# Weight sums of the banded attention's gates in tiles of a pool, loaded sooner, and a difference of tokens formed later

## The chip, the cores and the metric

The kernel runs on one core of one Trainium2 chip. The metric is device microseconds (us) of one execution. TensorE (PE) multiplies, ScalarE (ACT) and VectorE (DVE) work element by element, GpSimd (POOL) mostly issues transfers that add to what is in memory, and SyncE (SP) issues the plain loads. Each engine works through its own instructions in a fixed order.

## The reference, cut to what matters

One decoder layer, for 512 tokens of width 1024. Three branches read the same normalised tokens, and each is scaled by a sigmoid gate that is a projection of those tokens too:

```
u = rms_norm(h, ln_mix_pre)
qa, ka, va, qb, kb, vb, qm, gl = split(u @ w_in)      # gl: 3 x 1024 gate columns
y_swa = banded attention with sinks (8 heads of 64, window 128, relative bias)
y_sb  = stick-breaking attention   (8 heads of 64)
y_mem = attention over 256 memory rows (4 heads of 128)
g = sigmoid(gl)
merged = g[0] * (y_swa @ w_swa) + g[1] * (y_sb @ w_sb) + g[2] * (y_mem @ w_mem)
h = h + rms_norm(merged @ w_out)
h = h + rms_norm(swiglu(rms_norm(h)))
```

The banded attention's softmax is taken over the 256 keys of two neighbouring blocks, with a maximum that includes the sink; the first block of tokens has no block before it, and its weights there are zero.

## The kernel before, in words

**Products.** Everything stays close to fp32. An operand is split into a rounded part `hi` and a remainder `lo`, and each product is three matmuls, hi·hi, lo·hi and hi·lo (`mm3`, L190, whose three lines are L192, L194 and L195). `hi` is a cast on ACT (L146, L149 with a sign), `lo` a subtraction on DVE (L147, L150). For a few weights `lo` is made by ACT (L170) and a transfer of POOL that adds the weights from memory to it (L171).

**The stream.** Weights of 128 rows by 1024 come in the order of a list of units (`Stream`). When unit k starts on PE, `ahead` (L67) issues the loads up to unit k+4 on SP, and the splits up to unit k+3. Raw weights lie in a ring of five tiles (`raw`), hi and lo in rings of four. With a load or a split a unit can carry further steps ("load", "after"). A list of matmuls is fed bit by bit between the steps of the attention: `dn.run(us)` emits so many us of it.

**The gates of the banded attention.** They are made with seven products in place of eight half-size ones. `quarter` (L451) computes for each half n of the columns the products p1, p2 and p4 with plain weights, and p5, p6, p3 and p7 with sums of weights: "s" (for p5, then with more added for p6, then for p3) and "t" (for p7). A sum is made in a raw tile: `q_raw` (L391) loads it on SP, and `q_plus` (L398) adds to it by a transfer of POOL. `add_two_groups` (L482) lists the 14 units in the order p1, p5, p2, p6, p7, p3, p4, each with n = 0 and 1, and hangs those loads and additions at units some places ahead. Names: qx and qy are PSUM tiles of these products, qw a sum's tile, qkp a product copied out of PSUM (L438).

**The right sides.** The products need differences of tokens too. `rights` (L504) is a generator. Its first part takes the sum of hi and lo of the tokens of both halves, and their difference, in four tiles fx (L515, L516, on DVE); its second part splits the differences back into n0h to n3l, in place; later parts make the right sides of p6, p7 and p4.

**The banded attention.** `swa_pair` (L935) does two heads, four times (c = 0 to 3). Scores are in PSUM. POOL sets the first 128 columns of w to a large negative number (L954); DVE adds the bias (L955 to L957), takes the maxima (L965) and combines them with the sink (L968); ACT takes the exponentials, four of 128x256 and one of 128x4 for each head; DVE divides (L973 to L977); PE transposes (L988), ACT and DVE copy the transposes out of PSUM (L990, L991), and PE multiplies by the values (ysw, L198). Beside pairs 0 and 1 runs the stick-breaking branch's product with its weights (br, L192 to L195, with a gate's multiplication at L645), beside the last pairs the query projection of the memory heads (qm, evacuated by ACT at L327), and behind them the gates' products.

The program's order on each engine follows from the order of the code, a scheduler's priorities and what is ready in its own account; the rows under the change show what came out.

Of the kernel before, what the change touches and what calls it, by code (L numbers as in the profile page):

```python
# [14 lines left out]
ALU = mybir.AluOpType  # L15
# [99 lines left out]
def tile_kernel(ctx, tc, a):  # L115
    nc = tc.nc

    base = ctx.enter_context(tc.tile_pool(name="base", bufs=1))
# [10 lines left out]
    def ck(name, dt=F32):  # L129
        return ckp.tile([P, 512], dt, tag="ck", name=name)  # L130
# [12 lines left out]
    def split(raw, hi, lo, sign=1.0):  # L143

        if sign == 1.0:
            ins = nc.scalar.copy(hi, raw)  # L146
            lows = nc.vector.tensor_tensor(lo, raw, hi.bitcast(F32), op=ALU.subtract)  # L147
        else:
            ins = nc.scalar.mul(hi, raw, sign)  # L149
            lows = nc.vector.scalar_tensor_tensor(lo, raw, sign, hi.bitcast(F32), op0=ALU.mult, op1=ALU.subtract)  # L150
        if "behind" in st:
            after(ins, st["behind"][0])
            after(lows, st["behind"][1])
        return ins
# [12 lines left out]
    def split_dma(raw, hi, lo, src):  # L167

        nc.scalar.copy(hi, raw)
        nc.scalar.mul(lo, hi.bitcast(F32), -1.0)  # L170
        nc.gpsimd.dma_start(like(lo, src), src, accum_op=ALU.add)  # L171

    def w_split(raw, n, src=None):
        uid[0] += 1
        hi = wp.tile([P, 1024], F32R, tag="hi", name=f"hi{uid[0]}", bufs=4)
        lo = wp.tile([P, 1024], F32R, tag="lo", name=f"lo{uid[0]}", bufs=4)
        if src is not None:
            split_dma(raw[:, :n], hi[:, :n], lo[:, :n], src)
            return hi, lo
        sign = 1.0  # L180
        if isinstance(raw, tuple):
            raw, sign = raw
        ins = split(raw[:, :n], hi[:, :n], lo[:, :n], sign)
        if "chain" in st:
            after(ins, st["chain"])
        return hi, lo

    dn = Stream(w_load, w_split)

    def mm3(out, l, r, start, stop, right_last=False):  # L190
# [9 lines left out]
    def cols(hl, o, n):  # L200
        return hl[0][:, o : o + n], hl[1][:, o : o + n]
# [3 lines left out]
    def after(ins, first):  # L205
        dep = mybir.DependencyInfo(mybir.DependencyClass.NoSync, mybir.DependencyReason.DATA)
        tc.add_manual_dep(ins.ins, first.ins.name, dep, reason="order")
# [171 lines left out]
    qw, qb_, qk = {}, {}, {}  # L379
# [8 lines left out]
    def q_src(b, n, f, j):  # L388
        c = 17 + 8 * b + 4 * f + 2 * n
        return a["w_p"][:, c : c + 2, 4 * j : 4 * j + 4].rearrange("p g k n -> p g (k n)")  # L390
# [7 lines left out]
    def q_plus(b, n, key, f, j):  # L398
        raw = qw[(b, n, key)]
        nc.gpsimd.dma_start(raw[:, :].rearrange("p (g m) -> p g m", g=2), q_src(b, n, f, j), accum_op=ALU.add)  # L400

    def q_got(b, n, p):
        key = {"p5": "s", "p6": "s", "p3": "s", "p7": "t"}.get(p, p)

        def got():
            if (b, n, key) not in qw:
                q_raw(b, n, key, *{"p1": (0, 0), "p2": (0, 1), "p4": (1, 1)}[p])
            raw = qw[(b, n, key)]
            return (raw, -1.0) if p == "p3" else raw

        return got
# [39 lines left out]
    def quarter(b, n, p):  # L451
        def gen(hi, lo):
            if p in ("p1", "p5", "p2"):
                bank = aps if p == "p5" or (b, p) == (SWA, "p2") else dps
                qb_[(b, n, TILE[p])] = bank(f"q{TILE[p]}{b}{n}")
            ps = qb_[(b, n, TILE[p])]
            for j in range(2):
                for k in range(4):
                    first = p in ("p1", "p5", "p2") and j == 0 and k == 0
                    mm3(  # L460
                        ps[:, j * 256 : (j + 1) * 256], cols((hi, lo), (j * 4 + k) * P, P), right_of(p, k), first, k == 3
                    )
                    yield 0.36
            q_end(b, n, p, ps)

        return gen
# [14 lines left out]

    def add_two_groups(b):  # L482

        order = [(n, p) for p in ("p1", "p5", "p2", "p6", "p7", "p3", "p4") for n in range(2)]
        base = len(dn.units)
        for n, p in order:
            if p in PLAIN:
                dn.add(q_src(b, n, *PLAIN[p]), 1024, quarter(b, n, p))
            else:
                dn.add(q_got(b, n, p), 1024, quarter(b, n, p))  # L490

        def load_with(unit, back, *args):
            dn.units[base + order.index(unit) - back]["load"].append(lambda: args[0](*args[1:]))

        for n in range(2):
            load_with((n, "p5"), 4, q_raw, b, n, "s", 1, 0)
            load_with((n, "p5"), 2, q_plus, b, n, "s", 1, 1)
            load_with((n, "p7"), 4, q_raw, b, n, "t", 1, 0)
            load_with((n, "p7"), 3, q_plus, b, n, "t", 0, 0)
        for n in range(2):  # L500
            for p, j in (("p5", 0), ("p6", 1)):
                dn.units[base + order.index((n, p))]["after"].append(lambda n=n, j=j: q_plus(b, n, "s", 0, j))

    def rights():  # L504

        x, y = {}, {}

        def part(p, k, src, sign):
            h, l = cols(right[p][k // 2], (k % 2) * 256, 256)
            split(src, h, l, sign)  # L510

        for k in range(4):
            x[k] = ck(f"fx{k}")
            a0, a1 = x[k][:, :256], x[k][:, 256:]
            nc.vector.tensor_tensor(x[k][:, :], u[k][0].bitcast(F32), u[k][1].bitcast(F32), op=ALU.add)  # L515
            nc.vector.tensor_tensor(a1, a1, a0, op=ALU.subtract)  # L516
        yield
        for k in range(4):
            split(x[k][:, 256:], u[k][0][:, 256:], u[k][1][:, 256:])
        dn.open()  # L520
        yield
        for p in ("p6", "p7", "p4"):
            right[p] = [(ck(f"{p}rh{c}", F32R), ck(f"{p}rl{c}", F32R)) for c in range(2)]
        for k in range(4):
            y[k] = ck(f"fy{k}")
            b1 = y[k][:, 256:]
            nc.vector.tensor_tensor(y[k][:, :], u[4 + k][0].bitcast(F32), u[4 + k][1].bitcast(F32), op=ALU.add)
            nc.vector.tensor_tensor(b1, x[k][:, 256:], b1, op=ALU.subtract)
            part("p6", k, b1, 1.0)
            yield  # L530
        for p, z in (("p7", x), ("p4", y)):
            for k in range(4):
                b0 = z[k][:, :256]
                nc.vector.tensor_tensor(b0, y[k][:, 256:], b0, op=ALU.add)
                part(p, k, b0, -1.0)
                if k % 2:
                    yield
# [125 lines left out]
    for h in range(2):  # L663
        for q in range(3):
            n = 3 if q < 2 else 2
# [30 lines left out]
    dn.mark("plain_end")  # L696
    dn.gate()
    add_two_groups(SWA)
    dn.mark(f"gates{SWA}")
    add_branch(SWA, 1, False)  # L700
# [122 lines left out]
    def band_bias():  # L823
        oh = ck("oh")
        nc.gpsimd.dma_start(oh[:32, :384], a["onehot"])
        rbt = ck("rbt")
        nc.gpsimd.dma_start(rbt[:32, :8], a["rel_bias"])
        wm = ck("wm")
        nc.gpsimd.dma_start(wm[:, :384], a["winmask"])

        rb16 = ck("rb16")
        nc.gpsimd.tensor_copy(
            rb16[:32, :P].rearrange("b (h j) -> b h j", h=8), rbt[:32, :8].unsqueeze(2).to_broadcast([32, 8, 16])
        )
        ps = aps("pbias")
        mm(ps[:, :384], rb16[:32, :P], oh[:32, :384], True, True)
        row = ck("brow")
        nc.vector.tensor_tensor(row[:, :384], ps[:, :384], wm[:, :384], op=ALU.add)
        scr = drm.tile([8, P * 384], F32, name="bscr")
        nc.gpsimd.dma_start(  # L840
            scr[:, :].rearrange("h (j m i) -> (h j) m i", j=16, m=8),
            row[:, :384].unsqueeze(1).to_broadcast([P, 8, 384]),
        )
        out = []
        for i in range(4):
            b = ck(f"bias{i}")
            src = scr[2 * i : 2 * i + 2, 127:383]
            src = bass.AP(src.tensor, src.offset, [[383, P], [P * 384, 2], [1, 256]])
            nc.gpsimd.dma_start(b[:, :].rearrange("p (h k) -> p h k", h=2), src)
            out.append(b)  # L850
        return out
# [189 lines left out]
    for h in range(8):  # L1041
        if h == 1:
            bias = band_bias()
# [6 lines left out]
    dn.open()  # L1050
    table("natural_log_exp_and_others")
    for c in range(4):
        for us in swa_pair(c, bias):
            dn.run(us)
        if c == 2:
            made = rights()
            next(made)
    dn.until("plain_end")
    for _ in made:
        dn.run(1.5)  # L1060
# [607 lines left out]
```

## Time and profile before

| | |
|---|---|
| median of 3 runs | 811.78 us (811.72 to 812.59) |
| profiled execution | 810.99 us |
| its span | 809.2 us |
| granted TensorE clock | 0.997 of 2.4 GHz |
| PE busy | 796.1 us, 98% of the span |
| DVE, ACT, POOL busy | 76%, 60%, 12% |

The span runs from the first to the last instruction that the trace holds; the profiled execution is 1.8 us longer than its span. A row of a timeline begins with the start within the span, then the time that the instruction (or xN of them) took; what stands in brackets is the idle time of the engine before it, and what ended it. The stretch that the change touches lies between 200 and 330 us.

### The profile page before, as it was taken

What the parts mean: (1) busy time and instruction counts of PE and PEld (TensorE: products, weight loads), DVE (VectorE), ACT (ScalarE), POOL (GpSimd) and SP (SyncE); (2) the same over time, 40 slices, a digit from 0 to 9 for tenths busy, and PEclk for the clock granted to TensorE, in tenths of its full rate; (3) what the DMA queues carried; (4) which work ended last, traced back from release to release, by engine and by line L of the source; (5) the groups of instructions that cost most, each with busy time, mean ns of one, the idle gap of its engine ahead of it and who ended that gap; (6) DMA issues with size and microseconds to landing.
All of it is one profiled execution on the core that took longest, in us unless ns stands there. A gap on an engine that the chain in (4) does not pass through costs nothing.

```text
span 809.2 us, 13115 instructions
## 1 busy us (share of the span) xinstructions
PE 796.1 (98%) x5011; PEld 711.2 (88%) x5011; DVE 611.8 (76%) x985; ACT 487.1 (60%) x882; POOL 93.2 (12%) x115
## 2 busy tenths in 40 slices
PE   9999999999999999999999999999999999999996
PEld 6899788878788789889988899999999999988885
DVE  6898678545267787696694869967676777898797
ACT  7466677666856574755562566654444444666573
POOL 1002110000211111100004200100000000205200
PEclk9999999999999999999999999999999999999998
DMA  9343455213877438705569925987777662759902
GB/s 312 124 147 104 134 165 158 78 52 95 171 152 157 78 80 211 179 1 157 168 235 317 220 50 142 275 208 200 192 174 196 176 168 83 178 133 224 207 1 104
DMA packets 45295, 125.57 MB, mean 155 GB/s; under 512 B 5008, under 2 KB 6560, under 8 KB 45232
## 3 DMA queue, kind: packets, MB, share of 16 engines
q1 hardware_dynamic: 32368, 88.30, 33.5%
q0 software_dynamic: 12432, 36.17, 24.9%
q8 instruction: 39, 0.64, 0.3%
q10 hardware_dynamic: 432, 0.27, 0.1%
q14 instruction: 24, 0.20, 0.1%
HBM read 121.04 MB, written 3.67 MB: 154 GB/s over the span
## 4 chain that ended last, share of the span: by engine, by line
PE 91%; DVE 4%; DMA 1%; ACT 1%; issue 1%; DVEq 0%; ACTq 0%
PE gx L195 5%; PE gx L192 5%; PE gx L194 5%; PE z L198 4%; PE br L194 3%; PE br L192 3%; PE br L195 3%; PE x L194 2%; PE x L192 2%; PE x L195 2%; PE gy L195 2%; PE gy L194 2%; PE gy L192 2%; PE g L192 2%; PE g L194 2%; PE mx L192 2%
## 5 line engine op out<-in xcount | busy, mean ns | idle before, releaser
L146 ACT CAST hi<-gw 128x1024 fp32r<-128x1024 f32 x77 | 79.8, 1048 | 81.4 <-DVE gw L1253 39.8
L147 DVE TENSOR_TENSOR lo<-gw,hi 128x1024 fp32r<-128x1024 f32 x77 | 93.6, 1223 | 34.0 <-ACT hi L146 33.9
L146 ACT CAST hi<-raw 128x1024 fp32r<-128x1024 f32 (+2 forms) x46 | 46.7, 1028 | 40.9 <-PE qb L194 11.3
L147 DVE TENSOR_TENSOR lo<-raw,hi 128x1024 fp32r<-128x1024 f32 (+2 forms) x46 | 55.8, 1217 | 12.5 <-ACT hi L146 12.3
L1235 POOL DMA_DIRECT2D gw<-in_w_gu x27 | 23.3, 897 | 190.6 <-DMA gw<-in_w_gu 91.0
L146 ACT CAST hi<-r 128x1024 fp32r<-128x1024 f32 (+1 forms) x24 | 23.6, 982 | 19.9 <-PE y L195 5.3
L194 PE MATMUL x<-lo,lh 128*128 128x512 f32 x88 | 34.2, 389 | 0.0
L192 PE MATMUL x<-hi,lh 128*128 128x512 f32 x88 | 34.2, 389 | 0.0
L195 PE MATMUL x<-hi,ll 128*128 128x512 f32 x88 | 34.1, 389 | 0.0
L147 DVE TENSOR_TENSOR lo<-r,hi 128x1024 fp32r<-128x1024 f32 (+1 forms) x24 | 27.2, 1133 | 3.8 <-ACT hi L146 3.7
L892 DVE SCALAR_TENSOR_TENSOR e<-z,e 128x384 f32<-128x384 f32 (+1 forms) x24 | 14.4, 599 | 20.0 <-ACT e L211 20.0
L147 DVE TENSOR_TENSOR lo<-qw,hi 128x1024 fp32r<-128x1024 f32 x18 | 22.0, 1220 | 8.9 <-ACT hi L146 8.9
L211 ACT ACTIVATE e<-e 128x384 f32<-128x384 f32 (+1 forms) x48 | 26.9, 561 | 1.5
L400 POOL DMA_DIRECT2D qw<-in_w_p x12 | 14.5, 1245 | 114.8 <-DVE lo L147 34.7
L146 ACT CAST hi<-qw 128x1024 fp32r<-128x1024 f32 x18 | 18.9, 1050 | 14.1 <-PE qx L194 3.6
L146 ACT CAST hi<-bp 128x512 fp32r<-128x512 f32 x33 | 19.2, 620 | 13.5 <-PE y L195 4.8
L195 PE MATMUL gx<-N2h,lo 128*128 128x256 f32 x88 | 25.0, 284 | 0.3 <-DVE lo L147 0.3
L192 PE MATMUL gx<-B11h,hi 128*128 128x256 f32 x88 | 25.1, 285 | 0.2 <-ACT B11h L1164 0.2
L147 DVE TENSOR_TENSOR lo<-bp,hi 128x512 fp32r<-128x512 f32 x33 | 21.5, 686 | 4.7 <-ACT hi L146 4.5
L192 PE MATMUL mx<-woh,mgh 128*128 128x512 f32 x64 | 25.0, 391 | 0.0
L195 PE MATMUL gw<-B21h,lo 128*128 128x256 f32 x88 | 25.0, 284 | 0.0
L194 PE MATMUL gx<-B11l,hi 128*128 128x256 f32 x88 | 25.0, 284 | 0.0
(924 smaller groups left out, 3042.3 us busy)
## 6 DMA issues: line engine op xcount, KB each, us to landing
gw<-in_w_gu SPq DMA_DIRECT2D x57, 512.0 KB, 5.2
raw<-in_w_p SPq DMA_DIRECT2D x28, 512.0 KB, 4.3
gw<-in_w_gu POOLq DMA_DIRECT2D x27, 512.0 KB, 7.3
qw<-in_w_p SPq DMA_DIRECT2D x14, 512.0 KB, 4.6
raw<-in_w_br SPq DMA_DIRECT2D x12, 512.0 KB, 4.2
qw<-in_w_p POOLq DMA_DIRECT2D x12, 512.0 KB, 6.1
bp<-in_w_dn SPq DMA_DIRECT2D x22, 256.0 KB, 8.4
r<-in_w_dn POOLq DMA_DIRECT2D x10, 512.0 KB, 8.4
```

Of the source, the lines that this page charges most:

```text
L146: ins = nc.scalar.copy(hi, raw)
L147: lows = nc.vector.tensor_tensor(lo, raw, hi.bitcast(F32), op=ALU.subtract)
L192: one = nc.tensor.matmul(out, lh, rh, start=start, stop=False, skip_group_check=True)
L194: nc.tensor.matmul(out, *two, start=False, stop=False, skip_group_check=True)
L195: return one, nc.tensor.matmul(out, *three, start=False, stop=stop, skip_group_check=True)
L198: return nc.tensor.matmul(out, l, r, start=start, stop=stop, skip_group_check=True)
L211: ins = nc.scalar.activation(*args, **kw)
L400: nc.gpsimd.dma_start(raw[:, :].rearrange("p (g m) -> p g m", g=2), q_src(b, n, f, j), accum_op=ALU.add)
L892: nc.vector.scalar_tensor_tensor(x, z[i][:, :n], 0.0, x, op0=ALU.max, op1=ALU.add)
L1235: nc.gpsimd.dma_start(gw[(n, key)][:, :], g_src(n, i, j), accum_op=ALU.add)
```

## The change

The units of the banded gates come in the order (0,p1), (1,p1), (0,p2), (0,p5), (1,p5), (1,p2), then as before. The sum "s" of each half lies in two 128x512 tiles of the general pool (`ck`) instead of one 128x1024 tile of the raw ring; its loads, additions and splits are two each, of half the size. They are issued one unit (load) and two units (first addition) further ahead of p5. `rights()` is begun after the softmax of the last pair was emitted, not after pair c = 2. `w_split` takes a list of tiles.

```
--- before.py
+++ after.py
@@ -180,7 +180,11 @@
         sign = 1.0
         if isinstance(raw, tuple):
             raw, sign = raw
-        ins = split(raw[:, :n], hi[:, :n], lo[:, :n], sign)
+        if isinstance(raw, list):
+            for i, x in enumerate(raw):
+                ins = split(x[:, :], hi[:, i * 512 : (i + 1) * 512], lo[:, i * 512 : (i + 1) * 512], sign)
+        else:
+            ins = split(raw[:, :n], hi[:, :n], lo[:, :n], sign)
         if "chain" in st:
             after(ins, st["chain"])
         return hi, lo
@@ -481,7 +485,8 @@
 
     def add_two_groups(b):
 
-        order = [(n, p) for p in ("p1", "p5", "p2", "p6", "p7", "p3", "p4") for n in range(2)]
+        order = [(0, "p1"), (1, "p1"), (0, "p2"), (0, "p5"), (1, "p5"), (1, "p2")]
+        order += [(n, p) for p in ("p6", "p7", "p3", "p4") for n in range(2)]
         base = len(dn.units)
         for n, p in order:
             if p in PLAIN:
@@ -492,14 +497,22 @@
         def load_with(unit, back, *args):
             dn.units[base + order.index(unit) - back]["load"].append(lambda: args[0](*args[1:]))
 
+        def s_raw(n):
+            qw[(b, n, "s")] = [ck(f"qs{b}{n}{g}") for g in range(2)]
+            for g, t in enumerate(qw[(b, n, "s")]):
+                nc.sync.dma_start(t[:, :], q_src(b, n, 1, 0)[:, g])
+
+        def s_plus(n, f, j):
+            for g, t in enumerate(qw[(b, n, "s")]):
+                nc.gpsimd.dma_start(t[:, :], q_src(b, n, f, j)[:, g], accum_op=ALU.add)
+
         for n in range(2):
-            load_with((n, "p5"), 4, q_raw, b, n, "s", 1, 0)
-            load_with((n, "p5"), 2, q_plus, b, n, "s", 1, 1)
+            load_with((n, "p5"), 5, s_raw, n)
+            load_with((n, "p5"), 4, s_plus, n, 1, 1)
             load_with((n, "p7"), 4, q_raw, b, n, "t", 1, 0)
             load_with((n, "p7"), 3, q_plus, b, n, "t", 0, 0)
-        for n in range(2):
             for p, j in (("p5", 0), ("p6", 1)):
-                dn.units[base + order.index((n, p))]["after"].append(lambda n=n, j=j: q_plus(b, n, "s", 0, j))
+                dn.units[base + order.index((n, p))]["after"].append(lambda n=n, j=j: s_plus(n, 0, j))
 
     def rights():
 
@@ -1050,11 +1063,11 @@
     dn.open()
     table("natural_log_exp_and_others")
     for c in range(4):
-        for us in swa_pair(c, bias):
+        for i, us in enumerate(swa_pair(c, bias)):
+            if (c, i) == (3, 0):
+                made = rights()
+                next(made)
             dn.run(us)
-        if c == 2:
-            made = rights()
-            next(made)
     dn.until("plain_end")
     for _ in made:
         dn.run(1.5)
```

On SP, the plain loads, around the first sums. raw77 and raw80 of before are weights of the memory queries, qw76 and qw79 the two "s" sums of before, raw82 and raw84 of before and raw80 to raw84 of the change are plain weights of the gates, and qs000 to qs011 are the four tiles of the change. Before:

```order
L395 DMA qw76_2329<-in_w_p 128x2x512
L164 DMA raw77_2331<-in_w_p 128x1024
L395 DMA qw79_2445<-in_w_p 128x2x512
L164 DMA raw80_2447<-in_w_p 128x1024
L164 DMA raw82_2483<-in_w_p 128x2x512
L164 DMA raw84_2627<-in_w_p 128x2x512
```

After the change:

```order
L164 DMA raw80_2490<-in_w_p 128x2x512
L164 DMA raw82_2633<-in_w_p 128x2x512
L164 DMA raw84_2670<-in_w_p 128x2x512
L503 DMA qs000_2329<-in_w_p 128x512
L503 DMA qs001_2330<-in_w_p 128x512
L503 DMA qs010_2449<-in_w_p 128x512
L503 DMA qs011_2450<-in_w_p 128x512
```

The sums' loads, which stood between the weights of the memory queries, stand behind the plain weights of three gate products.

On POOL, at the same place. lo73 belongs to the branch's weights, lo75 to lo83 to the memory queries' weights; w10 and w50 are the masks of pair 1, w20 and w60 those of pair 2. Before:

```order
L171 DMA lo73_2236<-in_w_br 128x1024
L400 DMA qw79_2445<-in_w_p 128x2x512
L171 DMA lo75_2271<-in_w_p 128x1024
L171 DMA lo78_2334<-in_w_p 128x1024
L954 MEMSET w10_2381 128x128
L954 MEMSET w50_2404 128x128
L171 DMA lo81_2450<-in_w_p 128x1024
L171 DMA lo83_2486<-in_w_p 128x1024
```

After the change:

```order
L171 DMA lo73_2236<-in_w_br 128x1024
L171 DMA lo75_2271<-in_w_p 128x1024
L171 DMA lo77_2336<-in_w_p 128x1024
L507 DMA qs000_2329<-in_w_p 128x512
L507 DMA qs001_2330<-in_w_p 128x512
L967 MEMSET w10_2383 128x128
L967 MEMSET w50_2406 128x128
L507 DMA qs010_2449<-in_w_p 128x512
L507 DMA qs011_2450<-in_w_p 128x512
L171 DMA lo79_2456<-in_w_p 128x1024
L404 DMA qw87_2906<-in_w_p 128x2x512
```

The first additions, which stood well ahead of the masks of pair 1 (qw76's still before lo71), are now two, directly ahead of them, and two more follow.

On ACT, at the softmax of the last pair (heads 3 and 7). es3, w30 and w31 belong to head 3, es7, w70 and w71 to head 7; each row of w is two exponentials; n0h to n3h are casts of the tokens' differences, hi90 is the cast of a sum's tile qw79, qm2 and qm3 are the memory queries taken out of PSUM. Before:

```order
L146 CAST n0h_376<-fx0_2732 128x256
L146 CAST n1h_381<-fx1_2735 128x256
L146 CAST n2h_386<-fx2_2738 128x256
L146 CAST n3h_391<-fx3_2741 128x256
L146 CAST hi90_2903<-qw79_2445 128x1024
L211 ACTIVATE es3_2772<-nm3_2770,sinks_363 128x4
L327 ACTIVATE qm2_2810<-qm2_2668 128x512
L211 ACTIVATE w30_2764,den3_2771<-w30_2764,nm3_2770 128x256 x2
L211 ACTIVATE w31_2765,den3_2771<-w31_2765,nm3_2770 128x256 x2
L211 ACTIVATE es7_2795<-nm7_2793,sinks_363 128x4
L211 ACTIVATE w70_2787,den7_2794<-w70_2787,nm7_2793 128x256 x2
L211 ACTIVATE w71_2788,den7_2794<-w71_2788,nm7_2793 128x256 x2
```

After the change, where hi88 is cast from the sum's tiles qs000 and qs001:

```order
L215 ACTIVATE es3_2768<-nm3_2766,sinks_363 128x4
L215 ACTIVATE w30_2760,den3_2767<-w30_2760,nm3_2766 128x256 x2
L215 ACTIVATE w31_2761,den3_2767<-w31_2761,nm3_2766 128x256 x2
L146 CAST hi88_2908<-qs000_2329 128x512
L215 ACTIVATE es7_2791<-nm7_2789,sinks_363 128x4
L215 ACTIVATE w70_2783,den7_2790<-w70_2783,nm7_2789 128x256 x2
L215 ACTIVATE w71_2784,den7_2790<-w71_2784,nm7_2789 128x256 x2
L146 CAST n0h_376<-fx0_2806 128x256
L146 CAST hi88_2908<-qs001_2330 128x512
L331 ACTIVATE qm2_2818<-qm2_2676 128x512
L146 CAST n1h_381<-fx1_2809 128x256
```

The cast of the sum went from the place ahead of es3 to two places behind each head's exponentials, the evacuation of qm2 from right behind es3 to behind all of them, and the casts n0h to n3h, which stood ahead of all this, in between and after.

## Rows read from the trace of the kernel before

**Rows 1.** The page: busy time, share of the span and instructions of each engine
```profile
PE 796.1 (98%) x5011; PEld 711.2 (88%) x5011; DVE 611.8 (76%) x985; ACT 487.1 (60%) x882; POOL 93.2 (12%) x115
```

**Rows 2.** Waits of PE: engine, line waited for, total us, times, longest us
```profile
PE qx L192 <- ACT qm L327: 3.3, 2, 1.7
PE qx L192 <- ACT qkp L438: 0.6, 1, 0.6
```

**Rows 3.** Timeline of PE at the last pair, 279.5 to 294 us
```profile
280.60 0.38 PE L192 MATMUL qx<-n0h,hi 128*128 128x256 f32 x1 [1.59 <-ACT qm L327]
...
286.67 0.38 PE L192 MATMUL qx<-n0h,hi 128*128 128x256 f32 x1 [1.68 <-ACT qm L327]
...
293.05 0.28 PE L192 MATMUL qy<-n0h,hi 128*128 128x256 f32 x1
```

**Rows 4.** Timeline of DVE at the last pair, 270 to 282 us
```profile
272.71 0.68 DVE L515 TENSOR_TENSOR fx<-n0h,n0l 128x512 f32<-128x512 f32 x1
...
276.46 0.29 DVE L955 TENSOR_TENSOR w<-s,bias 128x128 f32<-128x128 f32 x1
...
278.97 0.22 DVE L968 TENSOR_SCALAR nm<-nm,sinks 128x4 f32<-128x4 f32 x1
```

**Rows 5.** Timeline of ACT at the last pair, 274 to 288 us
```profile
278.82 1.04 ACT L146 CAST hi<-qw 128x1024 fp32r<-128x1024 f32 x1 [1.78 <-PE qm L194]
279.77 0.29 ACT L211 ACTIVATE es<-nm,sinks 128x4 f32<-128x4 f32 x1
279.97 0.57 ACT L327 ACTIVATE qm<-qm 128x512 f32<-128x512 f32 x1
280.45 0.50 ACT L211 ACTIVATE w<-w,nm 128x256 f32<-128x256 f32 x1
...
286.03 0.59 ACT L327 ACTIVATE qm<-qm 128x512 f32<-128x512 f32 x1
```

**Rows 6.** Timeline of SP, 230 to 233 us
```profile
231.23 0.38 SPq L164 DMA_DIRECT2D raw<-in_w_p  x1
```

**Rows 7.** DMA issues begun from 53 to 56 us: count, KB each, median us to landing
```profile
mT<-in_memT SPq DMA_DIRECT2D x4, 256.0 KB, 5.5
```

**Rows 8.** DMA queues (packets, MB, share of 16 engines) and issues, 231 to 234 us
```profile
q0 software_dynamic: 123, 0.49, 96.0%
q1 hardware_dynamic: 4, 0.01, 1.1%
...
raw<-in_w_p SPq DMA_DIRECT2D x1, 512.0 KB, 5.8
lo<-in_w_p POOLq DMA_DIRECT2D x1, 512.0 KB, 8.7
```

**Rows 9.** Timeline of POOL, 200 to 310 us
```profile
232.94 0.85 POOL L171 DMA_DIRECT2D lo<-in_w_p  x1 [3.05 <-ACT lo L170]
233.48 0.67 POOL L954 MEMSET w<- 128x128 f32 x2
...
254.61 1.21 POOL L400 DMA_DIRECT2D qw<-in_w_p  x1 [4.87 <-DMA qw<-in_w_p]
```

**Rows 10.** Timeline of DVE, 236 to 257 us
```profile
238.00 0.68 DVE L965 TENSOR_REDUCE nm<-w 128x2 f32<-128x512 f32 x1
238.59 0.68 DVE L645 TENSOR_TENSOR g<-br,g 128x512 f32<-128x512 f32 x1
...
247.21 0.88 DVE L977 TENSOR_SCALAR w<-w,den 128x256 f32<-128x256 f32 x3
...
256.07 1.28 DVE L965 TENSOR_REDUCE nm<-w 128x2 f32<-128x512 f32 x2 [0.38 <-POOL w L954]
```

**Rows 11.** Timeline of PE at pair 1, 240.6 to 250 us
```profile
240.97 0.39 PE L192 MATMUL br<-y10h,hi 128*128 128x512 f32 x1
...
247.77 1.69 PE L988 MATMUL pt<-c_ident,w 128*128 128x128 f32 x14
```

**Rows 12.** Waits of ACT from 225 to 330 us
```profile
ACT hi L149 <- DMA qw<-in_w_p: 3.6, 2, 2.5
```

## The prediction, made before the changed kernel was run

> **What bounds the kernel now.** I read the page first: PE is busy 796.1 us, 98% of a span of 809.2 [rows 1]. A change that leaves the matmuls as they are can only touch PE's idle time, so the waits of PE come next. Near the change they are two waits for the evacuation of the memory queries, 3.3 us, and one for a product copied out of PSUM, 0.6 [rows 2]. Together they are 3.9 us, and no version of this change can give more than about that.
>
> The timeline of PE has the two large ones at the last pair: 1.59 us ahead of 280.60 and 1.68 ahead of 286.67; the gates' first products are then done at 293.05, where qy begins [rows 3]. The timelines of DVE and ACT say why. DVE spends 272.71 to 276.46, 3.75 us, on the tokens' difference fx and begins the last softmax only then [rows 4]. ACT meanwhile is held by the cast of a sum, which waits 1.78 for the last user of its hi tile, runs 278.82 to 279.77, and lets es and then the evacuation of qm (279.97) through; the next one follows at 286.03 behind all exponentials [rows 5].
>
> Everything here comes from one execution of 810.99 us, its span and 1.8 us around it. The median of the three runs is 811.78, 0.8 more; I add what the sum gives to 811.78. On this kernel about 0.2%, 1.6 us, is what can be told from no change.
>
> **The fx work behind the softmax: a gain.** Four sums and four subtractions leave the place ahead of the last softmax, which moves forward by up to 3.75: the first bias addition from 276.46 to 272.71, the first head's maxima (278.97 plus 0.22) to about 275.4 [rows 4]. The first head's four exponentials, 0.50 each [rows 5] and a short reading of the sum behind each, would end near 277.7. But in ACT's new order the cast hi88 of the first sum tile stands between the two heads, and its hi tile is free only when the third qm product is through, 278.8, as for the old cast [rows 5]. So es and the exponentials of the second head run from about 279.5 to 281.5, and the evacuation of qm2, now behind them and the second half of the cast, comes at 282.3 to 282.9 where it was 279.97 to 280.54. PE puts the seven transposes of the first head, formerly at 283.85, ahead of that wait and so has 0.9 us of work; then it idles, by these times, for 2.75 instead of the 1.59 of before. The second wait, 1.68, shrinks to about 0.35, since the evacuation of 286.03 no longer comes after its need. My account of PE's rows in the new order ends qx at 292.1 instead of 293.05 [rows 3]: **0.95 us gained**. Bounds: 3.27, if both waits go, and nothing, if qm2 comes another us later.
>
> **The sums, and p7.** The additions for p6 and p3 now come in halves, and DVE does its later steps some 1.5 us sooner. p7 of the first half waited 0.6 for a copy [rows 2], itself behind a cast that waited for a transfer, with another such cast close by: two waits on transfers, 3.6 together, the longest 2.5 [rows 12]. In the new order one cast moves ahead of the copies; since PE also has fourteen matmuls more before p7, I take a wait of about 0.25 instead of 0.6: **0.35 gained**, between 0.9 and a loss of 0.6 if the transfer that this cast waits for lands 1.2 later than I have it. Six casts and six subtractions of 1024 columns become twelve of 512, in which a fixed part of about 0.15 is paid once more each; all stand on engines with idle time there (ACT waited 3.6 for transfers alone [rows 12]), so I take 0. Without that cover they cost 0.9 on each of ACT and DVE. The two additions of 256 KB cost two issues of at least 0.85 on POOL instead of one of 1.21 [rows 9].
>
> **What the additions stand ahead of: a loss.** POOL works in order, and the first two additions are now directly ahead of the masks of pair 1. Before, these were set at 233.48, needed at 238.00 [rows 9, 10], and cost nobody anything. An addition cannot be issued until its own load has landed. The new loads stand on SP behind the plain load which before was issued at 231.23, when a raw tile came free [rows 6]; so the two for the first half leave at about 231.6 and 232.0, not at 203 and 218 as their forerunners.
>
> When does the second land? The plain load of 231.23 took 5.8, to 237.0: from 231 to 234 the additions held 96.0% of the transfer engines and the loads 1.1%, 123 packets against 4 [rows 8]. Four loads of 256 KB issued together landed in 5.5 [rows 7], about 0.65 after one another. Two more at that pace behind 237.0 give 238.3. If instead they share to the end with the addition issued at 232.94, which took 8.7 [rows 8, 9], the second takes as long, 232.4 plus 8.7, or 241.1. I take the middle, 239.7, as neither pace has a nearer row: the queue of additions is neither empty, as at 53 us, nor as full as at 231 throughout.
>
> From the landing to the mask: at 254.61 an addition began 0.6 after its load had landed, and the reduction that waited for the mask behind it began 1.46 later, at 256.07, itself 0.38 late for that reason [rows 9, 10]. It is this same order of instructions, once, in the kernel before. The smaller addition saves some 0.3, so the mask is there 1.7 to 2.0 after the landing: at 241.5, between 240.1 and 243.1. The reduction on DVE waits at 238.00 for it, and DVE stands. Behind it is the gate's multiplication of 238.59 which frees a bank of PSUM for the branch product that PE began at 240.97 [rows 10, 11]: it would end 1.3 after the mask, so that PE waits for whatever the mask is later than 239.7. The chain to the end of the weights' scaling (247.21 plus 0.88) is 9.8 when 0.3 of its idle time is taken up, and PE's last transposes, in the fourteen that begin at 247.77, have 1.1 of slack [rows 10, 11]; that is late from 239.4 on. The two waits are one shift: 241.5 less 239.4, **2.1 us lost**; from 0.7 at the early end to 3.7 at the late one. Pair 2's masks stand behind an addition too, as before: there I take 0, since the matmuls of its pair had about 1.6 of slack and the delay is some 1.2; at the late end 0.5.
>
> By the Trainium skill, "DMA: Bandwidth & Descriptors", section "Queues, rings and completion order", each transfer engine takes turns between the queues it has work for, packet by packet. The trace does not show that from 231 to 234 (123 packets against 4, [rows 8]). By the rule, the loads and the addition of 232.94 would share to their end, which is the late landing; by the row, the loads wait and then go quickly, which is nearer the early one.
>
> **The sum.** 0.95 and 0.35 gained, 2.1 lost: 0.8 to 0.9 us slower, 811.9 in the profiled execution's account and **812.6 us** for the median. With the loss between 0.7 and 3.7 and the gains between 0.4 and 1.9, its own range is 810.6 to 814.8.
>
> **The rivals.**
> - *The loads land late.* The loss decides once the mask comes later than about 242.3, which is a landing after 240.5: 3.5 lost and 0.5 at pair 2, less 1.3 gained, gives 814.5, slower. For it: 8.7 for a transfer issued in that very stretch [rows 8]. Against it: the load beside it took 5.8.
> - *The masks hold nobody.* If the mask is there by 239.4, only the gains stay: 811.78 less 1.3, 810.5, not slower. It needs a landing by 237.5, about 5.3 after the issue, as the four at 53 us had [rows 7]. Against it: the load ahead of them landed at 237.0 by itself.
> - *All waits vanish.* If besides ACT lets the evacuation of qm2 through in time, 3.9 go: 807.9. For it: the softmax does start 3.75 sooner. Against it: hi88 stands between the heads and its tile comes free only at 278.8.
> - *The change does not do what it says.* The sums are loaded sooner in units of the list, but, by SP's rows, later in time: this is a part of my forecast, not of a rival.
>
> **How the numbers follow.** Forecast 0.53, late loads 0.24, masks that hold nobody 0.15, all waits gone 0.08. Of the forecast nearly all lies within 0.2% (810.2 to 813.4), with 0.04 beyond on the slow side; of the late loads four fifths lie beyond; of the third case a third, where the gain is at its upper bound. Faster 0.08 + 0.05, about 0.14; slower 0.04 + 0.20, about 0.24; within 0.62. The range leaves out the case of all waits gone and the ends of the others: 810.0 to 814.7.
>
> **What the profile after would show.** Right: DVE waits for POOL's mask at pair 1 for some 3 us; PE waits near 241 for the bank, or for the transposes near 248, about 2 us in all; one wait for qm of 2 to 3 us at the last pair instead of two. Wrong: the sums' loads land before 237.5, or DVE's reduction at pair 1 waits for nothing; ACT evacuates qm2 by 280.5 on the old clock; or a new wait of PE stands at p5, where the cast of the halves comes late, which I have at nothing.

## The result, and the profile after

The changed kernel takes 814.91 us (median of 13 runs, 812.21 to 817.37), the kernel before 811.53 in the same 13 rounds (811.02 to 812.68): a ratio of 1.0039, 95% interval 1.0028 to 1.0051. It is 3.2 us slower. The profiled execution took 813.79, with a span of 812.0; of the 13 runs those with a mean clock of 0.996, as this one, took 812.21 to 814.91 us, those with 0.992 to 0.994 took 814.73 to 817.37. In the changed kernel all lines behind L183 have moved: mm3's three are L196, L198 and L199, the masks L967, the maxima L978, the gate's multiplication L658.

The waits of PE, in the columns of [rows 2]:

```profile
PE br L196 <- DVE g L658: 2.8, 1, 2.8
PE qx L196 <- ACT qm L331: 2.7, 1, 2.7
...
PE qx L196 <- ACT qkp L442: 0.2, 1, 0.2
```

Against [rows 2], the two waits for qm became one, the one at p7 nearly went, and a new one of 2.8 us came first. Its cause is read in four timelines. SP, where the four loads of the sums now stand together:

```profile
231.47 2.39 SPq L503 DMA_DIRECT2D qs<-in_w_p  x4
```

POOL, where the second addition waits for its load and the masks for the addition (compare [rows 9], masks at 233.48):

```profile
238.65 0.85 POOL L507 DMA_DIRECT2D qs<-in_w_p  x1 [5.07 <-DMA qs<-in_w_p]
241.30 0.85 POOL L507 DMA_DIRECT2D qs<-in_w_p  x1 [1.81 <-DMA qs<-in_w_p]
241.84 0.67 POOL L967 MEMSET w<- 128x128 f32 x2
```

DVE, whose maxima wait 4.54 us for the mask, with the gate's multiplication behind them (238.00 and 238.59 in [rows 10]):

```profile
242.40 0.69 DVE L978 TENSOR_REDUCE nm<-w 128x2 f32<-128x512 f32 x1 [4.54 <-POOL w L967]
243.00 0.68 DVE L658 TENSOR_TENSOR g<-br,g 128x512 f32<-128x512 f32 x1
```

PE, which waits for that multiplication's bank (240.97 in [rows 11]), and then works with longer matmuls:

```profile
240.07 0.39 PE L196 MATMUL br<-y13h,hi 128*128 128x512 f32 x1
...
243.74 0.50 PE L196 MATMUL br<-y10h,hi 128*128 128x512 f32 x1 [2.83 <-DVE g L658]
...
246.51 0.63 PE L196 MATMUL br<-y13h,hi 128*128 128x512 f32 x1
...
250.93 0.39 PE L196 MATMUL qm<-n0h,hi 128*128 128x512 f32 x1
```

The windows of one us say what the longer matmuls are (stretch, us, PE busy with its matmuls, granted clock, share of the transfer engines, GB/s): for a while after the idle time the clock is still at its upper level, 2.4 GHz, and then for some three us at half of it, 1.2 GHz.

```profile
244.00:245.00 1.00, 1.00 (x5) 1.00 0.93 156
245.00:246.00 1.00, 1.00 (x4) 0.61 0.71 90
246.00:247.00 1.00, 1.00 (x4) 0.50 1.02 176
...
248.00:249.00 1.00, 1.00 (x4) 0.68 0.61 109
249.00:250.00 1.00, 1.00 (x6) 1.00 0.70 139
```

Three rows of PE before, for the same instructions, make the account:

```profile
240.29 0.39 PE L192 MATMUL br<-y13h,hi 128*128 128x512 f32 x1
...
246.41 0.39 PE L192 MATMUL qm<-n0h,hi 128*128 128x512 f32 x1
...
328.44 0.28 PE L192 MATMUL ms<-mks0h,qms0h 128*128 128x256 f32 x1
```

The changed kernel is 0.22 us ahead at y13h (240.07), 2.77 behind at br<-y10h (243.74 against 240.97), 4.52 behind at qm<-n0h, and 2.93 behind where the memory scores begin, ms at 331.37:

```profile
331.37 0.28 PE L196 MATMUL ms<-mks0h,qms0h 128*128 128x256 f32 x1
```

So in these two executions the wait costs 2.99, the lower clock behind it 1.75, and everything from there to the memory scores, the last pair and the gates among it, gives back 1.59.

### The profile page after: what moved, and what is told of

Read it like the earlier page. It is cut to its first block, busy times and chain, and to the rows that moved or that the text cites. A ratio compares the mean times of both kernels' runs of the same rounds, so it can differ in the third digit from the quotient of the medians.

```text
span 812.0 us, 13149 instructions
## 1 busy us (share of the span) xinstructions
PE 797.1 (98%) x5011; PEld 712.1 (88%) x5011; DVE 611.6 (75%) x991; ACT 487.9 (60%) x888; POOL 96.6 (12%) x121
## 4 chain that ended last, share of the span: by engine, by line
PE 91%; DVE 4%; ACT 2%; DMA 2%; issue 1%; SPq 0%; DVEq 0%; POOL 0%; POOLq 0%; ACTq 0%
PE gx L199 5%; PE gx L196 5%; PE gx L198 5%; PE z L202 3%; PE br L196 3%; PE br L198 3%; PE br L199 2%; PE x L198 2%; PE x L196 2%; PE x L199 2%; PE gy L199 2%; PE gy L198 2%; PE gy L196 2%; PE g L196 2%; PE g L198 2%; PE mx L196 2%
## 5 line engine op out<-in xcount | busy, mean ns | idle before, releaser
L146 ACT CAST hi<-gw 128x1024 fp32r<-128x1024 f32 x77 | 79.8, 1048 | 81.4 <-DVE gw L1266 39.8
L198 PE MATMUL x<-lo,lh 128*128 128x512 f32 x88 | 34.2, 389 | 0.0
L196 PE MATMUL x<-hi,lh 128*128 128x512 f32 x88 | 34.2, 389 | 0.0
L199 PE MATMUL x<-hi,ll 128*128 128x512 f32 x88 | 34.1, 389 | 0.0
L199 PE MATMUL gx<-N2h,lo 128*128 128x256 f32 x88 | 25.0, 284 | 0.3 <-DVE lo L147 0.3
L196 PE MATMUL gx<-B11h,hi 128*128 128x256 f32 x88 | 25.1, 285 | 0.2 <-ACT B11h L1177 0.2
L196 PE MATMUL mx<-woh,mgh 128*128 128x512 f32 x64 | 25.0, 391 | 0.0
L199 PE MATMUL gw<-B21h,lo 128*128 128x256 f32 x88 | 25.0, 284 | 0.0
L198 PE MATMUL gx<-B11l,hi 128*128 128x256 f32 x88 | 25.0, 284 | 0.0
L199 PE MATMUL mx<-woh,mgl 128*128 128x512 f32 x64 | 24.9, 389 | 0.0
L199 PE MATMUL gy<-T1h,lo 128*128 128x256 f32 x88 | 24.9, 283 | 0.0
L196 PE MATMUL gy<-N22h,hi 128*128 128x256 f32 x88 | 24.9, 283 | 0.0
```

The source lines that it names most:

```text
L196: one = nc.tensor.matmul(out, lh, rh, start=start, stop=False, skip_group_check=True)
L198: nc.tensor.matmul(out, *two, start=False, stop=False, skip_group_check=True)
L199: return one, nc.tensor.matmul(out, *three, start=False, stop=stop, skip_group_check=True)
```

## The experiments

My theory after the result: POOL's fixed order puts pair 1's masks behind two additions whose loads land late; PE's wait for that, and the clock that falls behind it, are the whole loss; what is left of the change is a gain. The rival: the halved, later sums cost something themselves. Each time is a median; each ratio, with its 95% interval, is against the kernel before in the same rounds.

**e1: the masks set by DVE.**

```diff
-            nc.gpsimd.memset(w[h][0][:, :P], NEG)
+            nc.vector.memset(w[h][0][:, :P], NEG)
```

> The changed kernel with one edit: DVE sets the masks of the softmax, not POOL. My theory (the masks of pair 1 stand on POOL behind two additions whose loads land late; PE waits 2.8 us for that and then runs some us at half clock): DVE's wait of 4.5 us for POOL and PE's wait of 2.8 us at the bank go, and the granted clock stays 1.00 from 240 to 250 us. About 4.5 us come back, but in this order a table load stands ahead of the evacuation of qm2, so PE's wait there grows from 2.7 by about 1.3: about 811.7 us. Rival (the smaller, later transfers themselves slow the stretch): the time stays at 814 to 815.

812.25 us, 1.0003 (0.9995 to 1.0011). The wait at the bank is gone and the clock from 240 to 250 us is 1.00; the loss of 3.2 us went with it, as the theory has it. The second part came otherwise than I wrote: not qm but the scaling of the second head's weights is waited for, and the clock falls behind that (0.56 from 284 to 286 us).

```profile
PE pt L1001 <- DVE w L990: 3.6, 2, 3.4
```

**e2: only the difference of tokens moved** (the last hunk of the change, applied to the kernel before).

> The kernel before with only the difference of tokens moved behind the last softmax. My theory: no wait at pair 1 at all, one wait of 2.5 to 3 us for qm instead of two of 3.3 together, the second one gone: 0.5 to 1.3 us faster than before, about 810.6 us. Rival (the gain of 1.6 us that the changed kernel shows behind pair 2 belongs to the sums): no faster than before, 811.5 us.

811.22 us, 0.9992 (0.9983 to 1.0002): between the two numbers that I had set, at best a small gain; the interval just holds no change. PE's waits are the ones expected:

```profile
PE qx L192 <- ACT qm L327: 2.6, 1, 2.6
...
PE qx L192 <- ACT qkp L438: 1.0, 1, 1.0
```

3.3 us of waits for qm became 2.6, and 0.6 at p7 became 1.0: the softmax that starts 3.75 us sooner gives nearly nothing by itself.

**e3: only the sums' part** (the change without its last hunk).

> The changed kernel with the difference of tokens back ahead of the last softmax, so that only the sums' part is left. My theory: the wait at pair 1 and the half clock behind it are all there, the two waits for qm are back: 815.5 to 816.5 us. Rival (the loss comes from both parts together): at most 813.5 us.

821.47 us, 1.0117 (1.0099 to 1.0136), 5 us more than I expected; the direction is the theory's, the size is not. Its waits:

```profile
PE br L196 <- DVE g L658: 4.4, 1, 4.4
PE pt L1001 <- DVE w L990: 2.2, 3, 1.3
PE qx L196 <- ACT qkp L442: 2.2, 1, 2.2
PE qx L196 <- ACT qm L331: 1.7, 1, 1.7
```

The mask is later still, and two further waits, at the transposes and at p7, come on top; e7 has them too, without a late mask. That opened the rival again, which e7 takes up.

**e4: the first half's loads hung one unit further ahead** (the second half's stay at 5, so that "each" in the text below says too much).

```diff
-            load_with((n, "p5"), 5, s_raw, n)
+            load_with((n, "p5"), 6 - n, s_raw, n)
```

> The changed kernel with one number changed: the sums' loads are hung one unit further ahead (6 instead of 5 ahead of each p5). On SP the first half's two loads then stand ahead of two plain loads, and on POOL its additions two places further ahead of the masks of pair 1. My theory: the masks wait for nothing that is late, DVE's wait of 4.5 us goes, the clock stays at 1.00, and the gains behind pair 2 stay: 810 to 810.5 us. Rival (additions on POOL ahead of the masks cost as such, or their issue does): 813 us or more.

811.47 us, 0.9988 (0.9977 to 0.9999): a gain of 1.0 us by the ratio (0.1 to 1.9), while the median lies 1 us above the range that I gave. POOL now has:

```profile
223.42 1.73 POOL L507 DMA_DIRECT2D qs<-in_w_p  x2 [2.54 <-DVE nm L978]
...
233.39 0.67 POOL L967 MEMSET w<- 128x128 f32 x2
```

The masks are back at 233.4, with the same number of additions ahead of them and POOL still in charge of them: the additions ahead of the masks cost nothing here, since their loads have landed. This and e1 show the cause of the loss from two sides. What it does not show is the full gain: the one wait for qm (2.67 us) is followed by half clock in this profile, where the profile of the change, with the same wait, kept 1.00.

```profile
280.00:282.00 2.00, 0.20 (x2) 0.93 0.00 0
282.00:284.00 2.00, 1.13 (x5) 0.50 0.00 0
...
286.00:288.00 2.00, 2.00 (x12) 0.50 0.00 0
```

Its 12 runs lie accordingly: the three with a mean clock of 0.997 or 0.998 took 809.14 to 809.49 us, the five with 0.994 or 0.995 811.72 to 812.17, and the four between, with 0.996, 810.79 to 812.11.

**e5: the second head's exponentials and the sums' casts ordered behind the evacuation of qm2** (on e4; `after` only sets an order). In `proj`, and likewise behind each cast in `w_split`'s new loop, `after(ins, st[("evac", "qm", 2)])`:

```diff
-                        nc.scalar.mul(t[:, :], ps[:, :], s)
+                        st[("evac", kind, idx)] = nc.scalar.mul(t[:, :], ps[:, :], s)
+                        if (kind, idx) == ("qm", 2):
+                            after(st[("es", 7)], st[("evac", kind, idx)])
```

> The kernel with the loads hung one unit further ahead (as e4_load_earlier), and ACT's order changed by two order-only dependencies: the second head's exponentials of the last pair and the casts of the sums come behind the evacuation of qm2. My theory (the one wait of 2.7 us that is left is ACT's order, and whether the clock falls behind it is what makes executions differ by 3 us): the wait for qm shrinks to 0.5 us or less, the granted clock stays at 1.00 from 280 to 290 us in the profile, the runs lie within 1.5 us of one another, 807 to 807.8 us. Rival (the evacuation is late because PSUM is filled late, or the waits go to the scaling of the second head's weights): a wait of 2 us or more at another place, 809 us or more.

811.13 us, 0.9995 (0.9986 to 1.0004): missed. ACT's timeline says why:

```profile
278.62 0.41 ACT L146 CAST n0h<-fx 128x256 fp32r<-128x256 f32 x1 [1.09 <-PE qm L199]
281.21 0.41 ACT L146 CAST n1h<-fx 128x256 fp32r<-128x256 f32 x1 [2.19 <-DVE fx L532]
281.52 0.59 ACT L332 ACTIVATE qm<-qm 128x512 f32<-128x512 f32 x1
```

The casts of the differences slipped ahead of the evacuation and waited for DVE; PE waited 2.1 us for qm, with half clock behind it, and 1.4 at p7.

**e6: the same order with the old sums** (e2 with e5's dependency on the exponentials).

> The kernel before with the difference of tokens behind the last softmax and the second head's exponentials behind the evacuation of qm2, the sums as before. My theory: the cast of the old sum tile, which waits for the last qm product, still stands ahead of the evacuation, so a wait of 0.3 to 0.8 us for qm stays, and the one of 1.0 us at p7: about 808.7 us. If the sums in pool tiles are what gives the gain instead: 810.5 us or more.

811.07 us, 0.9987 (0.9978 to 0.9996). Two waits for qm, 2.03 and 0.75; the one at p7 is below the view. My theory's number, 808.7, was missed: the casts of the differences stand ahead here too. The time lies where I had put the case that the sums in pool tiles give the gain, 810.5 us or more, but that does not follow: e4 and e5, with pool tiles, have ratios of 0.9988 and 0.9995 and are no faster than this.

**e7: only the sums' part, with the loads 6 units ahead** (e3 with e4's edit).

> As e3_sums_only (the sums' part without the difference of tokens moved), with the loads hung 6 units ahead instead of 5. If all of the 10 us that e3 lost come from the masks behind late additions and what follows from it (the clock, the later additions shifted): 811 to 811.5 us, the two waits for qm of 3.3 us as before. Rival (the sums in halves cost some us by themselves when DVE and ACT are late): 814 us or more.

815.15 us, 1.0037 (1.0024 to 1.0049): the rival's time. No wait at pair 1, and still 3 us lost:

```profile
PE qx L196 <- ACT qkp L442: 2.3, 1, 2.3
PE pt L1001 <- DVE w L990: 1.7, 2, 1.3
PE qx L196 <- ACT qm L331: 1.7, 1, 1.7
```

The wait at p7 is on ACT, where the cast of a half stands ahead of the copy that PE needs, and waits for its addition:

```profile
315.21 0.63 ACT L149 ACTIVATE hi<-qs 128x512 fp32r<-128x512 f32 x1 [2.29 <-DMA qs<-in_w_p]
315.75 0.57 ACT L442 COPY qkp<-qy 128x512 f32<-128x512 f32 x1
```

In e4 the same cast waits 1.66 us, and PE waits 0.2 at p7. In e7 the clock also falls to half, from 288 to 290 us behind waits of 1.7 and 1.3, and from 318 to 320 behind the one at p7. So the sums' part costs 3 us where the difference of tokens stands at its old place, and nothing that these runs can tell where it has moved. The two parts of the change are not a sum. Whether it is the halves that cost this, or the new order of the units, which e7 has too, no run separates.

**e8: the kernel before with the masks on DVE.**

> The kernel before with the masks set by DVE, nothing else: a control for e1. Two settings a pair lie on DVE's path to the softmax instead of POOL's, and DVE's wait of 0.4 us for POOL at pair 2 goes: 811 to 812 us, no change that can be measured. If DVE's settings cost more than that, e1 hid a larger gain.

811.31 us, 0.9994 (0.9985 to 1.0003). The masks cost DVE nothing that can be measured; e1 hid no gain.

**e9: the casts n0h to n3h behind the evacuation too** (on e5).

```diff
-            split(x[k][:, 256:], u[k][0][:, 256:], u[k][1][:, 256:])
+            after(split(x[k][:, 256:], u[k][0][:, 256:], u[k][1][:, 256:]), st[("evac", "qm", 2)])
```

> As e5_qm2_ahead, and the casts n0h to n3h are also ordered behind the evacuation of qm2 (in e5 they stood ahead of it and waited for DVE's differences, which kept PE waiting 2.1 us). My theory: ACT evacuates qm2 right behind the first head's exponentials, near 277.5 us, before PE needs it; PE has no wait of more than 0.6 us between 270 and 300 us and the clock stays at 1.00 there; 807.3 to 808.5 us, in a spread under 2 us. Rival (something else, the scaling of the second head's weights or the evacuation of qm3, takes the wait over): 810 us or more.

812.20 us, 1.0006 (0.9998 to 1.0015). There is no wait for qm any more, and no gain. The time came back behind it:

```profile
PE qx L197 <- ACT qkp L445: 1.9, 1, 1.9
...
PE qy L200 <- DVE lo L150: 1.2, 1, 1.2
PE qx L197 <- ACT p6rh L146: 0.9, 1, 0.9
```

PE, without the wait of 2.7 us that e4 still had, waits at p6, qy and p7 instead, and behind p7 the clock is at half from 316 to 318 us. PE is at p7 only 0.4 us sooner than in e4; the copy that it waits for there ran at 313.88, in e4 at 312.56, so the chain itself came later too, and why is not shown. It is the expected rival, though at other places than I named. The runs spread by 3.1 us, not under 2.

**e10: the same order with the old sums.**

> The kernel before with the difference of tokens behind the last softmax and the same orders on ACT as in e9 (second head's exponentials, casts of differences and of weights behind the evacuation of qm2), but the sums in the raw ring as before. If the sums in pool tiles bring nothing of their own, as I now hold: 807.5 to 809 us, within 0.7 us of e9. If they bring what the halves were to bring at p7: e9 is faster by 1 us or more.

813.30 us, 1.0014 (1.0005 to 1.0023), 4 us above my range; 2.9 us of waits at qy and 1.3 at qw. By the ratios 0.7 us lies between e9 and e10, less than the 1 us that I had set for a gain of the halves' own; a small one in this order of ACT stays open.

**e11 and e12: the difference of tokens formed on POOL.** With e7's sums, and with the old ones and the masks on DVE:

```diff
-            nc.vector.tensor_tensor(x[k][:, :], u[k][0].bitcast(F32), u[k][1].bitcast(F32), op=ALU.add)
-            nc.vector.tensor_tensor(a1, a1, a0, op=ALU.subtract)
+            nc.gpsimd.tensor_tensor(x[k][:, :], u[k][0].bitcast(F32), u[k][1].bitcast(F32), op=ALU.add)
+            nc.gpsimd.tensor_tensor(a1, a1, a0, op=ALU.subtract)
```

> As e7_sums_only_earlier (sums in pool tiles, loads hung 6 units ahead, the tokens' difference at its old place ahead of the last softmax), with the difference formed on POOL, not on DVE. If e9 moved its waits to p6, qy and p7 because DVE and ACT, not PE, bound the stretch from 280 to 315 us, taking 3.75 us of work from DVE there must shorten it: no wait of PE over 0.6 us from 270 to 300 us, the waits at p6, qy and p7 under 1.5 us together, 808 to 809.5 us. Rival (the additions of the sums, a chain of cast, transfer, cast, bound it): waits of 2 us or more at p6 to p7 as in e9, 810.5 us or more.

> The kernel before with the difference of tokens formed on POOL and the masks on DVE (which cost nothing in e8), the sums as before. On POOL the difference stands behind an addition that the kernel before issues only at 272 us, so the casts of the differences on ACT, ahead of the softmax's exponentials, come up to 6 us late: 811 to 814 us. If it is not held there, the same as e11 within 1 us, and the sums in pool tiles bring nothing of their own.

816.16 us, 1.0050 (1.0037 to 1.0062), and 813.08, 1.0019 (1.0010 to 1.0028). Both lose, for a reason that I had not thought of and that is told below: in e11 it made PE wait 1.4 and 2.0 us near 268 and 271, with half clock behind it, so e11 does not settle DVE's load as I meant it to. What it does show: with no wait for qm at the last pair and DVE relieved of 3.75 us there, the waits behind it are still 1.17 (qy) and 1.15 (p7), 1.17 and 1.91 in e9. That speaks for the chain of cast, addition and cast as what bounds the stretch from qy to p7, and does not prove it. e12 came out in its first range, since the difference started at 272.9.

No version clearly beats the kernel before; the best are e6 and e4, 1.0 us ahead by the ratio, with intervals that just leave out no change.

## Why the prediction was right and where it was wrong

The sign, the place and the mechanism up to PE's wait were right; the size was not, and the mechanism had no clock in it. The forecast was 812.6, 0.8 to 0.9 us slower. The median is 814.9, and by the ratio the change is 3.2 us (2.3 to 4.1) slower, which from the kernel before in the same rounds gives 814.7, the very end of the range. The sum's own range was added wrongly: 811.78 with 3.7 lost and 0.4 gained is 815.1, not 814.8. The rival "the loads land late" is what happened, but that its 814.5 comes so near is in part luck: it had 3.5 for the wait and 0.5 at pair 2, where 2.99 and nothing were measured, and no term for the clock, 1.75.

- *What the additions stand ahead of.* Forecast: DVE waits for the mask for some 3 us, PE about 2.1. Measured: 4.54 and 2.99, with the mask there at 242.4 instead of 241.5; the rival's condition, "later than about 242.3", was met. From the mask on the prediction's own step holds: 242.4 less 239.4 is 3.0. The step that failed is the landing: the middle of two paces, 239.7, where the second addition began at 241.30, 0.6 after a landing by the prediction's own step, so at 240.7. (The late pace, 241.1, was counted from 232.4, though the prediction has the second load leave at 232.0.) From 231 to 234 us the additions had 86.7% of the transfer engines and the loads 3.4%, 122 packets against 8, much as before:

```profile
q0 software_dynamic: 122, 0.47, 86.7%
q1 hardware_dynamic: 8, 0.02, 3.4%
...
qs<-in_w_p SPq DMA_DIRECT2D x4, 256.0 KB, 8.8
```

  By the turns between queues of the Trainium skill ("DMA: Bandwidth & Descriptors", section "Queues, rings and completion order") the loads would have had a fair share of these packets; the trace shows no such share in these 3 us, again. Afterwards the two changed places: from 234 to 236 the loads had 91.7% (281 packets against 13), and from 238 to 240, with the first half's own addition issued at 238.65, the additions had 79.8% and the loads 23.5%. So the landing came near the one that I had worked out for the rule, but not for its reason: additions held the loads back twice, with a free stretch between. [rows 8] had 8.7 us for a transfer of POOL issued there, and I took the middle instead of it.
- *What the wait does to the clock.* The sum had no term for it; in the profiled execution it cost 1.75 us, more than the whole forecast. The waits of the kernel before, up to 1.68 us, left the clock at 1.00, so no row of it gave this term a size. But the prediction took it at nothing without saying so, although it forecast a longer wait, and no bound of its range has it.
- *The fx work behind the softmax*, and *the sums, and p7*. Together 1.30 forecast, 1.59 measured in the changed kernel's profile and 1.0 (0.1 to 1.9) in e4's runs, the wait for qm 2.67 where I had 2.75. But the split of 0.95 and 0.35 is not confirmed: e2 gives the first part 0.6 (-0.2 to 1.4), and e7 makes the second a loss of 3.0 (1.9 to 4.0) by itself. That the sum came near is luck: it rested on two parts that need each other, which I did not see.
- *Pair 2's masks*: taken at 0; DVE waited 0.19 there, PE not at all.
- *All waits vanish*: e9 made the case with its condition met, the evacuation in time, and it did not give 3.9 us (ratio 1.0006). The bound from [rows 2] was taken for what would be gained; it is that only if nobody is late behind it, and ACT and DVE were.

## What to carry to other kernels

When transfers are moved on an engine that issues in order, look at what small instruction now stands behind them, and ask when their own source lands, not when they are listed. A load "sooner" in a list can be later in time when its queue stands on a buffer: here 231.47 us instead of 203 and 218. And a wait of PE that goes is only worth what is left when the next supplier is asked: here two orders of ACT (e9, e10) each removed the wait for qm, and PE waited elsewhere 16 to 32 us later.

## What the runs showed of the hardware that I had not expected

- **An operation of DVE stood still while POOL computed.** In e11 the operation of 128x4 that takes 0.22 us in [rows 4] took 6.48, until POOL's additions and subtractions were through; in e12, at another place, 6.14. DVE's and POOL's timelines of e11:

```profile
256.79 0.28 DVE L968 TENSOR_TENSOR w<-s,bias 128x128 f32<-128x128 f32 x1
256.98 6.48 DVE L981 TENSOR_SCALAR nm<-nm,sinks 128x4 f32<-128x4 f32 x1
263.38 0.41 DVE L969 TENSOR_TENSOR w<-s,bias 128x256 f32<-128x256 f32 x1
```

```profile
255.17 1.79 POOL L528 TENSOR_TENSOR fx<-n0h,n0l 128x512 f32<-128x512 f32 x1
...
261.56 1.88 POOL L529 TENSOR_TENSOR fx<-fx 128x256 f32<-128x256 f32 x2
```

  DVE's bias addition at 256.79 ran beside POOL, the small operation did not until the last of POOL's ended at 263.44. The Trainium skill ("GPSIMD Engine Reference", section "1. Specifications") says that the two share their interfaces to SBUF and contend for some kinds of DVE operations; the trace agrees that they do, and shows one operation held not for one instruction of POOL but until the last of its eight sums and subtractions had ended.
- **The clock after a wait.** PE's waits of 1.59 and 1.68 us at the last pair left the clock at 1.00 in the profile before; so did 2.08 in e8, 2.58 in e2 and 2.67 in the changed kernel. But half clock followed 2.67 in e4, 2.09 in e5 and 2.03 in e6, and in e7 waits of 1.68 and 1.29 that ended 6 us apart. So the length of the last wait alone does not tell whether the clock falls, and these runs do not show what does. Where it fell, a wait cost more than its length: 2.99 and another 1.75 at pair 1 of the changed kernel. In e4 the runs with the lower mean clock are mostly the longer ones, over a spread of 3 us. In e5 and e9 runs at 0.998 and 0.999 took 812.58 and 812.84 us, others at 0.995 811.08 to 813.21, so the clock is not all of that spread.
